# FFN-in with the high weights in one 512-column matmul per k-tile, and one pool of PSUM banks

## The chip, the cores and the metric

The kernel runs on one core of a Trainium2 chip. The metric is the device time of one execution in microseconds (us), the median of several runs. TensorE (PE) multiplies, and its weight loads have a row of their own (PEld); VectorE (DVE) and ScalarE (ACT) do the elementwise work, GpSimd (POOL) a little of it, and the queue of SyncE (SP) issues the transfers from device memory. PSUM, where matmuls accumulate, has 8 banks; a bank holds 512 fp32 values for each of 128 partitions.

## The reference

Two layers, each `x + FFN`, a mixer, and `x + FFN` again, on 256 tokens of 1024 channels in fp32. What the change touches is the first product of the four feed-forward stages (two per layer, `ffa` and `ffb`):

```
def swiglu(h, w_in, w_out):                      # h [256, 1024], w_in [1024, 2*2816], w_out [2816, 1024]
    gate, up = jnp.split(h @ w_in, 2, axis=-1)
    return (jax.nn.silu(gate) * up) @ w_out
...
x = x + 0.5 * swiglu(rms_norm(x, ffa_norm[l]), ffa_w_in[l], ffa_w_out[l])
```

The mixer between them runs three branches (a low-rank attention, a gated delta rule with a causal convolution, a block attention), gates them and projects them back.

## The kernel before

Each fp32 product is made of three fp32r matmuls. A weight block of 512 KB is loaded into `raw`, ACT casts it to its high part `wh` (line 258, two casts of 512 columns) and DVE subtracts to get the low part `wl` (line 259); the activations are kept as high and low parts as well, in tiles [128, k-tile, part, token]. A product is then high x high, high x low and low x high.

There are two forms of the product. `chunk` (lines 278 to 280) is token-major: 128 tokens are the stationary operand, the weights stream through in 512 columns. It makes the first 512 gate columns of each FFN, FFN-out, and many mixer products. `tiles` (lines 306 to 308) is channel-major: a 128x128 piece of the weights is stationary, the 256 tokens stream. It makes all other columns of FFN-in, 20 tiles of 256 columns per feed-forward stage with 8 k-tiles each, and the mixer's gates and branches. One PSUM bank holds the whole tile, two column halves (`c`) of 256 tokens. Its three matmuls per column half and k-tile have 256 columns each:

```
mm(o, wh[:, k, v], xh, ...)     # L306
mm(o, wh[:, k, v], xl, ...)     # L307
mm(o, wl[:, k, v], xh, ...)     # L308
```

The mixer's convolution tiles (lines 914 and 915) already have the other form: `wh` streams against the high and the low tokens in one matmul of 512 columns, `wl` against the high tokens in one of 256, and the two halves of the bank are added at eviction, an ACT copy (line 924) and a DVE add (line 926).

In FFN-in a gate tile is evicted by `silu2`: ACT's tanh from the bank (line 428) and a DVE operation on both (line 429). An up tile is multiplied by its gate from the bank (DVE, line 460), then split by an ACT cast (line 324) and a DVE subtraction (line 325), which gives `HT[j]` for FFN-out.

The PSUM banks are three pools: `acc` with 3 banks for the weights' products, `pm` with 3 for attention and the delta rule, `tp` with 2 for transposes. `held` counts the banks in use: `acc()` lets other chains go first until fewer than 3 are held, `hold()` keeps chains of `pm` below 2. The order of the work is the order of emission, taken as the priority by a scheduler that places the instructions on each engine; chains beside the weights are generators that yield for a number of events. Weights are split at least LEAD = 3 steps ahead, and 7 pairs `wh`, `wl` exist.

Of the kernel before, what the change touches and what calls it, by code (L numbers as in the profile page):

```python
# [8 lines left out]
F32 = mybir.dt.float32  # L9
# [27 lines left out]
NACC, NTP = 3, 2  # L37
# for how many events a chain lets others go first
Y_ATT, Y_INV, Y_DMA, LAG, START, G_AHEAD = 3, 3, 8, 2, 40, 20
# the mixer's weights: L low-rank products, C conv channels, M block attention, Z delta rule's z, G gates, B branches  # L40
# [32 lines left out]
class Step:  # L73
    """One group of weights: load() -> (DRAM blocks, k-tiles, columns), use(t, wh, wl) per token half;
    joint: used once, for both halves, by a generator."""
# [5 lines left out]
class Kern:  # L81
    def __init__(self, ctx, tc, ins, out):
        self.tc, self.nc, self.ins, self.out = tc, tc.nc, ins, out
        self.sb = ctx.enter_context(tc.tile_pool(name="sb", bufs=1))
        self.dr = ctx.enter_context(tc.tile_pool(name="dr", bufs=1, space=bass.MemoryType.DRAM))
        self.ps = ctx.enter_context(tc.tile_pool(name="ps", bufs=1, space=bass.MemoryType.PSUM))
        self.n = 0
        self.gens, self.clock = [], 0
        self.held = {"acc": 0, "pm": 0}

# [16 lines left out]
    def pm(self):  # L107
        return self.ps.tile([128, 512], F32, name=self.nm("pm"), tag="pm", bufs=8 - NACC - NTP)

    def acc(self):  # L110
        """a bank for the weights' products; its last reader calls done("acc")"""
        self.until(lambda: self.held["acc"] < NACC)
        self.held["acc"] += 1
        return self.ps.tile([128, 512], F32, name=self.nm("acc"), tag="acc", bufs=NACC)

    def hold(self):
        """a chain that keeps a bank over a yield first waits for this, and ends with done("pm")"""
        while self.held["pm"] >= 7 - NACC - NTP:
            yield 1
        self.held["pm"] += 1  # L120
# [5 lines left out]
    # A generator is a chain of work beside the weights; it yields, for so many events, where its  # L126
    # next piece has to wait for another engine.
# [55 lines left out]
    def layer_params(self, l):  # L183
# [12 lines left out]
        # rope tables with the gains folded in: [t][A | B]  # L196
# [39 lines left out]
    def fetch(self, split, most=NRAW):  # L236
        """start the loads that have room; split one more k-tile pair's half, if it is not far ahead"""
# [27 lines left out]
    def chunk(self, src, nk, n, xget, epi, before=None):  # L265
        """[tokens, n] = x @ w, token-major, per token half; src(k0, k1) -> DRAM blocks."""
# [19 lines left out]
    def tiles(self, w, nk, a0, both, epi, before=None):  # L286
        """256 columns of x @ w, channel-major, both token halves at once: bank [128, 2 column tiles, 256 tokens]"""
        acc = []

        def step(g):  # L290
# [3 lines left out]
            def use(wh, wl):  # L294
# [6 lines left out]
                for c in range(2):  # L301
                    o = ps[:, c * 256:(c + 1) * 256]
                    v = slice(c * 128, (c + 1) * 128)
                    for k in range(4):
                        xh, xl = both(4 * g + k)
                        mm(o, wh[:, k, v], xh, start=(g == 0 and c == 0 and k == 0), stop=False, skip_group_check=True)  # L306
                        mm(o, wh[:, k, v], xl, start=False, stop=False, skip_group_check=True)  # L307
                        mm(o, wl[:, k, v], xh, start=False, stop=(4 * g + k == nk - 1), skip_group_check=True)  # L308
                    if c == 0:
                        yield  # L310
# [16 lines left out]
    def rsq(self, out, ss, add, mul=1.0):  # L327
        """out = (mul * ss + add) ** -0.5"""
# [11 lines left out]
    def half_T(self, n):  # L340
        """storage for n k-tiles of one token half, split: (tile, dst)"""
# [12 lines left out]
    def norm(self, t, gain, put, lag):  # L354
        """rms norm of x's half t, transposed and split; put(c, y) does that for 512 channels"""
# [33 lines left out]
    def xboth(self, k):  # L389
        for t in range(NH):  # L390
            self.until(lambda: (t, k // 4) in self.XR)
        return self.X[k // 2][:, k % 2, 0, :], self.X[k // 2][:, k % 2, 1, :]
# [22 lines left out]
    def ffn(self, l, name, norm_after):  # L415
# [9 lines left out]
        def silu2(dst, ps):  # L425
            """dst = 2 * silu(ps)"""
# [5 lines left out]
        def epi_first(t, ps):  # L432
            """the first 512 gates come token-major, for each half of the tokens"""
# [13 lines left out]

        def epi_gate(j):
            def f(ps):
                SG[j] = self.b2().rearrange("p (k c) -> p k c", k=2)  # L450
                silu2(SG[j], ps)
                self.done("acc")
                return
                yield
            return f

        def epi_up(j):
            def f(ps):
                h = self.b2().rearrange("p (k c) -> p k c", k=2)
                nc.vector.tensor_tensor(h, SG[j], ps.rearrange("p (k c) -> p k c", k=2), op=OP.mult)  # L460
                self.done("acc")
# [17 lines left out]
    def rope(self, dst, src, tab, H, d):  # L479
        """dst = src * A + swap(src) * B over H heads; src may be in PSUM"""  # L480
# [9 lines left out]
    def sumsq(self, src):  # L490
        """sum of src[:, h, :] ** 2, by the scalar engine alone"""
# [85 lines left out]
    def gdn(self, ready, sil, beta, g, zs, oT):  # L577
        """the gated delta rule over two chunks of 128 tokens, four heads at once; sil(0..2): 2*silu of the conv of
        q, k, v, channel-major, there when ready(i)"""
# [41 lines left out]
        # The l2 norms of q and k stay factors of the token: with r = 1 / |k|, k = r k',  # L621
        # beta (1 + tril(beta k k^T D))^-1 (v - e k S) = beta r (1 + tril(k' k'^T D beta r^2))^-1 (v / r - e k' S)
# [65 lines left out]
        def invert(c):  # L688
# [46 lines left out]
            # the last level joins two blocks of 64  # L735
# [95 lines left out]
    def mixer(self, l, norm_after):  # L831
# [8 lines left out]
        # c_q, c_kv, k_rope, b, a  # L840
        def epi_c(t, ps):
# [37 lines left out]
            # g = -exp(a_log) * softplus(a + dt_bias), softplus(x) = max(x, 0) + log(1 + exp(-|x|))  # L879
# [19 lines left out]
        # q, k, v of the delta rule: channel-major, 128 channels at a time  # L899
        def conv_tile(i, h):  # L900
# [6 lines left out]
            def use(wh, wl):  # L907
# [4 lines left out]
                for k in range(8):  # L912
                    xh, xl = self.xboth(k)
# [26 lines left out]
        # low-rank attention: queries, then keys and values  # L940
# [54 lines left out]
        def use_kv(t, wh, wl):  # L995
            xh, xl = cget(t, 2)
            for hg in range(2):
                self.until(lambda: self.held["pm"] < 7 - NACC - NTP)
# [10 lines left out]
        def attend():  # L1009
            """both softmax branches, one after the other"""  # L1010
# [23 lines left out]
        # block attention: one block holds the whole sequence, so every routed block is masked and only the  # L1034
        # causal part in the block is left
# [30 lines left out]
        # gates, the delta rule's z and the branches  # L1066
# [19 lines left out]
        def gates(n):  # L1086
            r = []
            for j in range(4):
                r += self.tiles(w_in, 8, GATE + n * D + j * 256, self.xboth, epi_gate(n, j))
# [19 lines left out]
        def branch(n):  # L1109
            r = []  # L1110
            both = lambda k: (d["oT", n][k // 2][:, k % 2, 0, :], d["oT", n][k // 2][:, k % 2, 1, :])
            for j in range(4):
                r += self.tiles(ins["w_branch"][l, n], 4, j * 256, both, epi_b(n, j),
# [20 lines left out]
    def phase(self, steps):  # L1134
        """the first half of the tokens runs SKEW steps ahead of the second"""
        n = len(steps)
        ev = [(0, i) for i in range(SKEW)]
# [26 lines left out]
    def run(self):  # L1164
# [29 lines left out]
        with self.tc.manual_schedule():  # L1194
            # the first half's norm and the first weights, in the order in which they arrive
# [26 lines left out]
        for p in phases:  # L1222
            self.phase(p)
# [22 lines left out]
```

## Time and profile before

| | |
|---|---|
| median of 3 runs | 1360.8 us (1360.14 to 1361.75) |
| span of the profiled execution, first to last instruction | 1358.5 us |
| PE / PEld busy | 1333.1 us (98%) / 1218.3 us (90%) |
| DVE / ACT / POOL busy | 881.6 (65%) / 734.3 (54%) / 122.4 us (9%) |
| data moved by the DMA engines | 231.39 MB, mean 170 GB/s |
| granted TensorE clock | full speed in all 40 slices |

The profile gives the profiled execution's span and no other time of it; the median is 2.3 us above that span. Matmuls are pipelined: the duration of one (283 ns for 256 columns) runs on while the next ones have started, so the rate is read from the distance of two starts. Busy PE is the union of these durations, so it is high wherever PE is fed at all. Idle time of DVE and ACT costs nothing as long as PE does not wait for them.

### The profile page before, as it was taken

How to read it: one execution, taken by the hardware profiler on the slowest of the kernel's cores; microseconds unless marked ns; L12 is line 12 of the kernel's file. 1: busy time of each engine (PE TensorE's matmuls, PEld its weight loads, DVE VectorE, ACT ScalarE, POOL GpSimd, SP SyncE). 2: the span in 40 equal slices, each digit the busy share in tenths (PEclk: the TensorE clock that was granted, in tenths of full speed). 3: DMA queues.
4: the chain of work that ended last, by engine and by line, in shares of the span. 5: the costliest groups of instructions: out<-in, count | busy, mean ns of one | idle time of the engine just before them, and what ended most of it. 6: DMA issues, size and time to landing. Idle time of an engine off the chain costs nothing.

```text
span 1358.5 us, 23647 instructions
## 1 busy us (share of the span) xinstructions
PE 1333.1 (98%) x9066; PEld 1218.3 (90%) x9066; DVE 881.6 (65%) x1730; ACT 734.3 (54%) x1623; POOL 122.4 (9%) x157
## 2 busy tenths in 40 slices
PE   6999999999999999999999999999999999999998
PEld 5999888788899979998889998887889999899987
DVE  6666458898557676555575555588875576765552
ACT  6444447776655465444464444477757644644432
POOL 0010003711101000000000000044120000000000
PEclk9999999999999999999999999999999999999999
DMA  8866565566343656565666565555554445666552
GB/s 274 231 217 185 172 186 134 171 174 172 109 125 110 187 169 208 182 185 173 198 187 197 180 183 174 165 156 161 166 147 119 136 131 171 186 186 185 180 174 67
DMA packets 207568, 231.39 MB, mean 170 GB/s; under 512 B 15616, under 2 KB 166112, under 8 KB 207456
## 3 DMA queue, kind: packets, MB, share of 16 engines
q1 hardware_dynamic: 207456, 229.89, 56.7%
q8 instruction: 71, 1.16, 0.3%
q14 instruction: 41, 0.34, 0.1%
HBM read 227.11 MB, written 2.75 MB: 169 GB/s over the span
## 4 chain that ended last, share of the span: by engine, by line
PE 91%; DVE 3%; POOL 3%; ACT 1%; DMA 1%; issue 1%; SPq 0%; DVEq 0%; ACTq 0%; POOLq 0%
PE acc L306 16%; PE acc L307 16%; PE acc L308 16%; PE acc L278 10%; PE acc L280 10%; PE acc L279 10%; PE acc L914 3%; PE pm L523 2%; PE acc L915 1%; POOL s L331 1%; DMA raw<-in_ffa_w_in 1%; DVE wl L259 1%; POOL s L330 1%; PE tp L336 1%; PE pm L562 1%
## 5 line engine op out<-in xcount | busy, mean ns | idle before, releaser
L259 DVE TENSOR_TENSOR wl<-raw,wh 128x512 fp32r<-128x512 f32 (+1 forms) x844 | 555.7, 687 | 295.4 <-ACT wh L258 295.2
L258 ACT CAST wh<-raw 128x512 fp32r<-128x512 f32 (+1 forms) x844 | 487.9, 618 | 479.2 <-issue 323.4
L306 PE MATMUL acc<-q,wh 128*128 128x256 f32 x1856 | 530.3, 286 | 0.0
L307 PE MATMUL acc<-q,wh 128*128 128x256 f32 x1856 | 525.4, 283 | 2.0 <-DVE q L325 2.0
L308 PE MATMUL acc<-q,wl 128*128 128x256 f32 x1856 | 525.4, 283 | 0.0
L307 PEld LDWEIGHTS acc<-q,wh 128*128 128x128 f32 x1856 | 355.9, 192 | 3.7 <-DVE q L325 2.8
L306 PEld LDWEIGHTS acc<-q,wh 128*128 128x128 f32 x1856 | 355.9, 192 | 2.7 <-issue 1.0
L308 PEld LDWEIGHTS acc<-q,wl 128*128 128x128 f32 x1856 | 355.8, 192 | 0.0
L278 PE MATMUL acc<-wh,q 128*128 128x512 f32 (+2 forms) x656 | 258.4, 394 | 1.5 <-ACT q L324 1.4
L280 PE MATMUL acc<-wh,q 128*128 128x512 f32 (+2 forms) x656 | 255.8, 390 | 0.0
L279 PE MATMUL acc<-wl,q 128*128 128x512 f32 (+2 forms) x656 | 255.1, 389 | 0.0
L278 PEld LDWEIGHTS acc<-wh,q 128*128 128x128 f32 x656 | 123.7, 189 | 26.8 <-ACT q L324 2.4
L280 PEld LDWEIGHTS acc<-wh,q 128*128 128x128 f32 x656 | 123.5, 188 | 26.3 <-DVE q L325 2.1
L279 PEld LDWEIGHTS acc<-wl,q 128*128 128x128 f32 x656 | 123.6, 188 | 21.8
L914 PE MATMUL acc<-q,wh 128*128 128x512 f32 x192 | 70.9, 407 | 0.0
L358 POOL TENSOR_TENSOR s<-s,mhalf 128x1 f32<-128x1 f32 x12 | 8.3, 692 | 643.6 <-DVE s L351 643.6
L915 PE MATMUL acc<-q,wl 128*128 128x256 f32 x192 | 54.0, 281 | 0.0
L460 DVE TENSOR_TENSOR d<-d,acc 128x512 f32<-128x512 f32 x36 | 24.8, 688 | 41.9 <-PE acc L308 41.9
L914 PEld LDWEIGHTS acc<-q,wh 128*128 128x128 f32 x192 | 36.1, 188 | 8.6 <-issue 0.7
L535 ACT ACTIVATE d<-pm,s,s 128x128 f32<-128x128 f32 (+1 forms) x64 | 32.1, 509 | 21.2 <-DVE s L531 20.6
L331 POOL TENSOR_TENSOR s<-s,mhalf 128x4 f32<-128x4 f32 (+2 forms) x32 | 36.9, 1155 | 2.5
L915 PEld LDWEIGHTS acc<-q,wl 128*128 128x128 f32 x192 | 36.3, 189 | 0.4
(197 smaller groups left out, 1066.5 us busy)
## 6 DMA issues: line engine op xcount, KB each, us to landing
raw<-in_w_in SPq DMA_DIRECT2D x104, 512.0 KB
raw<-in_ffa_w_in SPq DMA_DIRECT2D x88, 512.0 KB
raw<-in_ffb_w_in SPq DMA_DIRECT2D x88, 512.0 KB
raw<-in_ffa_w_out SPq DMA_DIRECT2D x44, 512.0 KB
raw<-in_ffb_w_out SPq DMA_DIRECT2D x44, 512.0 KB
raw<-in_w_branch SPq DMA_DIRECT2D x24, 512.0 KB
raw<-in_w_out SPq DMA_DIRECT2D x16, 512.0 KB
raw<-in_w_in SPq DMA_DIRECT2D x8, 416.0 KB
```

Of the source, the lines that this page charges most:

```text
L258: nc.scalar.copy(s.wh[:, v], s.raw[:, v])
L259: nc.vector.tensor_sub(s.wl[:, v], s.raw[:, v], s.wh[:, v].bitcast(F32))
L278: mm(o, xh, wh[:, j, :], start=(k == 0), stop=False)
L279: mm(o, xh, wl[:, j, :], start=False, stop=False)
L280: mm(o, xl, wh[:, j, :], start=False, stop=(k == nk - 1))
L306: mm(o, wh[:, k, v], xh, start=(g == 0 and c == 0 and k == 0), stop=False, skip_group_check=True)
L307: mm(o, wh[:, k, v], xl, start=False, stop=False, skip_group_check=True)
L308: mm(o, wl[:, k, v], xh, start=False, stop=(4 * g + k == nk - 1), skip_group_check=True)
L331: g.tensor_tensor(out, out, self.mhalf[:, 0:out.shape[-1]], op=OP.pow)
L535: nc.scalar.activation(P[:, h, :], ps[:, h, :], AF.Exp, scale=rqs[:, h:h + 1], bias=nb[:, h:h + 1], accum_out=sm[:, h:h + 1])
L914: mm(p, wh[:, k, :], self.X[k // 2][:, k % 2], start=(k == 0), stop=False, skip_group_check=True)
L915: mm(p[:, 0, :], wl[:, k, :], xh, start=False, stop=(k == 7), skip_group_check=True)
```

## The change

In FFN-in, `tiles` now uses two banks, one per column half. For each k-tile it issues one matmul of 512 columns, `wh` against high and low tokens, and one of 256 columns, `wl` against the high tokens into the bank's first half. A bank is evicted by the new `whole`: an ACT copy of its second half and, an event later, a DVE add of its first half. The gate's tanh and DVE operation and the up tile's multiplication then read SBUF. The old function stays as `narrow` for the mixer's gates and branches. `acc` and `pm` become one pool of 6 banks; up to 4 `acc` banks may be held in a feed-forward stage, 3 in the mixer, and 2 `pm` banks by `hold()` as before. The rest of the diff is comments taken out and the moving operand passed as one tile instead of two.

```
-NACC, NTP = 3, 2
+NTP = 2
+BANKS = 8 - NTP
     def pm(self):
-        return self.ps.tile([128, 512], F32, name=self.nm("pm"), tag="pm", bufs=8 - NACC - NTP)
+        return self.ps.tile([128, 512], F32, name=self.nm("pm"), tag="bank", bufs=BANKS)
     def acc(self):
-        self.until(lambda: self.held["acc"] < NACC)
+        self.until(lambda: self.held["acc"] < self.nacc)
         self.held["acc"] += 1
-        return self.ps.tile([128, 512], F32, name=self.nm("acc"), tag="acc", bufs=NACC)
+        return self.ps.tile([128, 512], F32, name=self.nm("acc"), tag="bank", bufs=BANKS)
     def hold(self):
-        while self.held["pm"] >= 7 - NACC - NTP:
+        while self.held["pm"] >= BANKS - 4:
...
     def tiles(self, w, nk, a0, both, epi, before=None):
+                for c in range(2):
+                    if g == 0:
+                        acc[c] = self.acc()
+                    ps = acc[c]
+                    v = slice(c * 128, (c + 1) * 128)
+                    for k in range(4):
+                        x2 = both(4 * g + k)
+                        last = 4 * g + k == nk - 1
+                        mm(ps.rearrange("p (s c) -> p s c", s=2), wh[:, k, v], x2, start=(g == 0 and k == 0), stop=False,
+                           skip_group_check=True)
+                        mm(ps[:, 0:256], wl[:, k, v], x2[:, 0, :], start=False, stop=last, skip_group_check=True)
+                    if 4 * g + 4 == nk:
+                        self.spawn(epi(c, ps))
+                    if c == 0:
+                        yield
...
+        def whole(dst, ps):
+            nc.scalar.copy(dst, ps[:, 256:512])
+            yield 1
+            nc.vector.tensor_tensor(dst, dst, ps[:, 0:256], op=OP.add)
+            self.done("acc")
         def epi_gate(j):
-            def f(ps):
-                SG[j] = self.b2().rearrange("p (k c) -> p k c", k=2)
-                silu2(SG[j], ps)
-                self.done("acc")
+            def f(c, ps):
+                if c == 0:
+                    SG["raw", j] = self.b2().rearrange("p (k c) -> p k c", k=2)
+                g = SG["raw", j]
+                yield from whole(g[:, c, :], ps)
+                if c == 1:
+                    yield 1
+                    SG[j] = self.b2().rearrange("p (k c) -> p k c", k=2)
+                    silu2(SG[j], g.rearrange("p k c -> p (k c)"))
         def epi_up(j):
-                nc.vector.tensor_tensor(h, SG[j], ps.rearrange("p (k c) -> p k c", k=2), op=OP.mult)
-                self.done("acc")
+                h = SG["up", j]
+                yield from whole(h[:, c, :], ps)
+                if c == 0:
+                    return
+                yield 1
+                while j not in SG:
+                    yield 1
+                nc.vector.tensor_tensor(h, h, SG[j], op=OP.mult)
...
-    def phase(self, steps):
+    def phase(self, steps, nacc):
...
-            self.phase(p)
+            self.phase(p, 3 if i % 3 == 1 else 4)
```

**On PE, inside FFN-in.** Before, at the border of two tiles of the first feed-forward stage (`acc_638` and `acc_705` are banks, `q_96` to `q_99` the tokens, `wh` and `wl` the weights' parts, in brackets the semaphores that a row waits for):

```order
L306 MATMUL acc_638<-q_99,wh_562 128x256
L307 MATMUL acc_638<-q_99,wh_562 128x256
L308 MATMUL acc_638<-q_99,wl_563 128x256
L306 MATMUL acc_705<-q_96,wh_598 128x256 [waits DVE_49]
L307 MATMUL acc_705<-q_96,wh_598 128x256
L308 MATMUL acc_705<-q_96,wl_599 128x256
```

The same border in the changed program:

```order
L309 MATMUL acc_710<-q_99,wh_635 128x512
L311 MATMUL acc_710<-q_99,wl_636 128x256
L309 MATMUL acc_757<-q_96,wh_663 128x512 [waits DVE_49]
L311 MATMUL acc_757<-q_96,wl_664 128x256
...
L309 MATMUL acc_814<-q_96,wh_663 128x512 [waits DVE_49]
L311 MATMUL acc_814<-q_96,wl_664 128x256
```

Three matmuls of a k-tile have become two, and a tile opens two banks instead of one, with a wait at the first matmul of each.

**On DVE, inside FFN-in.** Before, around an up tile (its multiplication is L460) and its split (L325):

```order
L460 TENSOR_TENSOR d_558<-d_487,acc_497 128x512 [waits DVE_49,PE_49]
L259 TENSOR_TENSOR wl_668<-raw_526,wh_667 128x512 [waits DMAHW3_49,Activation_49]
L259 TENSOR_TENSOR wl_668<-raw_526,wh_667 128x512 [waits Activation_49]
L325 TENSOR_TENSOR q_579<-d_558,q_579 128x2x256 [waits Activation_49]
L259 TENSOR_TENSOR wl_702<-raw_560,wh_701 128x512 [waits DMAHW5_49,PE_49,Activation_49]
```

The same in the changed program (L486 is the new add, L512 the multiplication, L359 the split, L261 the weights' low part):

```order
L486 TENSOR_TENSOR d_619<-d_619,acc_580 128x256 [waits Activation_49]
L261 TENSOR_TENSOR wl_726<-raw_605,wh_725 128x512 [waits DMAHW6_49,PE_49,Activation_49]
L486 TENSOR_TENSOR d_619<-d_619,acc_592 128x256 [waits Activation_49]
L261 TENSOR_TENSOR wl_726<-raw_605,wh_725 128x512 [waits Activation_49]
L512 TENSOR_TENSOR d_619<-d_619,d_601 128x512 [waits DVE_49]
L261 TENSOR_TENSOR wl_754<-raw_633,wh_753 128x512 [waits DMAHW0_49,PE_49,Activation_49]
L359 TENSOR_TENSOR q_675<-d_619,q_675 128x2x256 [waits Activation_49]
L261 TENSOR_TENSOR wl_754<-raw_633,wh_753 128x512 [waits Activation_49]
```

Two adds per tile have come between the subtractions, each behind an ACT copy.

**On PE, in the first mixer.** Before, the second token half of a 384-column product (`acc_2532`) stands inside another product and its first row waits:

```order
L280 MATMUL acc_2430<-wh_2363,q_2160 128x512
L278 MATMUL acc_2430<-wh_2403,q_2161 128x512
L278 MATMUL acc_2532<-wh_2442,q_2297 128x384 [waits DVE_49,PE_49]
L279 MATMUL acc_2532<-wl_2443,q_2297 128x384
L280 MATMUL acc_2532<-wh_2442,q_2297 128x384
...
L279 MATMUL acc_2430<-wl_2404,q_2161 128x512
L946 MATMUL tp_2540<-ident,d_2494 128x128 [waits DVE_49,Activation_49]
```

In the changed program its two halves follow each other, and the wait is at a later product (`acc_2374`):

```order
L282 MATMUL acc_2291<-wh_2123,q_2086 128x384
L280 MATMUL acc_2321<-wh_2231,q_2086 128x384
...
L282 MATMUL acc_2321<-wh_2231,q_2086 128x384
L280 MATMUL acc_2219<-wh_2152,q_1949 128x512
...
L280 MATMUL acc_2374<-wh_2266,q_1947 128x512 [waits PE_49]
L997 MATMUL tp_2329<-ident,d_2283 128x128 [waits DVE_49,Activation_49]
```

The pieces of work are the same and stand in another order; the mixer's PE list has 8 more rows with a wait than before (130 for 122 in the first mixer).

## Rows read from the trace of the kernel before

**Rows 1.** The head of the profile's page and the table of engines: busy time, share of the span, instructions; and the granted clock by fortieths of the span.
```profile
span 1358.5 us, 23647 instructions
PE 1333.1 (98%) x9066; PEld 1218.3 (90%) x9066; DVE 881.6 (65%) x1730; ACT 734.3 (54%) x1623; POOL 122.4 (9%) x157
PEclk9999999999999999999999999999999999999999
```

**Rows 2.** The costliest groups of instructions: line, engine, operation, tiles, shapes, count; then busy us, mean ns of one; then idle time of the engine before them.
```profile
L306 PE MATMUL acc<-q,wh 128*128 128x256 f32 x1856 | 530.3, 286 | 0.0
L307 PE MATMUL acc<-q,wh 128*128 128x256 f32 x1856 | 525.4, 283 | 2.0 <-DVE q L325 2.0
L308 PE MATMUL acc<-q,wl 128*128 128x256 f32 x1856 | 525.4, 283 | 0.0
L306 PEld LDWEIGHTS acc<-q,wh 128*128 128x128 f32 x1856 | 355.9, 192 | 2.7 <-issue 1.0
L914 PE MATMUL acc<-q,wh 128*128 128x512 f32 x192 | 70.9, 407 | 0.0
L915 PE MATMUL acc<-q,wl 128*128 128x256 f32 x192 | 54.0, 281 | 0.0
```

**Rows 3.** The timeline of PE in the first FFN-in, start in us, duration in us: the first and the last of 35 matmuls of 256 columns in unbroken order.
```profile
99.80 0.28 PE L306 MATMUL acc<-q,wh 128*128 128x256 f32 x1
...
103.88 0.28 PE L307 MATMUL acc<-q,wh 128*128 128x256 f32 x1
```

**Rows 4.** The timeline of PE in FFN-out of the first feed-forward stage: the first and the last of 15 matmuls of 512 columns in unbroken order.
```profile
169.67 0.39 PE L278 MATMUL acc<-wh,q 128*128 128x512 f32 x1
...
172.84 0.39 PE L280 MATMUL acc<-wh,q 128*128 128x512 f32 x1
```

**Rows 5.** The timeline of PE in a convolution tile of the first mixer, 8 pairs of a 512- and a 256-column matmul: the second pair's first matmul, the last pair's first, and the next product.
```profile
246.73 0.39 PE L914 MATMUL acc<-q,wh 128*128 128x512 f32 x1
246.96 0.28 PE L915 MATMUL acc<-q,wl 128*128 128x256 f32 x1
...
248.81 0.39 PE L914 MATMUL acc<-q,wh 128*128 128x512 f32 x1
249.04 0.28 PE L915 MATMUL acc<-q,wl 128*128 128x256 f32 x1
```

**Rows 6.** The same in another convolution tile, behind 256-column matmuls of the gates: the first and the last of its 8 pairs.
```profile
300.35 0.40 PE L914 MATMUL acc<-q,wh 128*128 128x512 f32 x1
300.58 0.28 PE L915 MATMUL acc<-q,wl 128*128 128x256 f32 x1
...
302.82 0.40 PE L914 MATMUL acc<-q,wh 128*128 128x512 f32 x1
```

**Rows 7.** Busy time of the engines in stretches that lie inside the FFN-in of the four feed-forward stages: stretch, its us, then busy us and count of PE, PEld, DVE, ACT, POOL, the granted clock, the DMA share and GB/s.
```profile
32.00:88.00 56.00, 56.00 (x469) 56.00 (x468) 36.64 (x61) 27.74 (x52) 7.61 (x18) 1.00 0.80 240
515.00:618.00 103.00, 103.00 (x861) 103.00 (x860) 62.91 (x100) 50.22 (x90) 0.00 (x0) 1.00 0.61 189
702.00:808.00 106.00, 106.00 (x886) 106.00 (x885) 64.99 (x103) 51.38 (x92) 0.00 (x0) 1.00 0.63 192
1182.00:1288.00 106.00, 106.00 (x886) 106.00 (x885) 64.97 (x103) 51.36 (x92) 0.00 (x0) 1.00 0.61 187
```

**Rows 8.** Groups of DVE and ACT in the stretch 515 to 618 us, with the idle time before them and what ended it.
```profile
L259 DVE TENSOR_TENSOR wl<-raw,wh 128x512 fp32r<-128x512 f32 x72 | 47.2, 687 | 30.2 <-ACT wh L258 30.2
L460 DVE TENSOR_TENSOR d<-d,acc 128x512 f32<-128x512 f32 x8 | 5.5, 688 | 8.1 <-PE acc L308 8.1
L258 ACT CAST wh<-raw 128x512 fp32r<-128x512 f32 x72 | 41.8, 618 | 53.1 <-issue 51.7 <-PE acc L307 1.4
```

**Rows 9.** The eviction of the convolution tiles, durations in ns, least, median and most.
```profile
L924 ACT COPY d<-acc x24: 348/367/411, 249.8 to 1081.5; 128x256 f32<-128x256 f32 x24
L926 DVE TENSOR_TENSOR d<-acc,d x24: 385/418/426, 252.4 to 1082.7; 128x256 f32<-128x256 f32 x24
```

**Rows 10.** What PE waited for, the whole span: us in total, times, longest us; and one stretch that holds most of the first mixer, with columns as in Rows 7.
```profile
PE tp L336 <- DVE d L362: 12.2, 8, 9.4
PE tp L946 <- DVE d L1057: 3.9, 4, 1.2
PE acc L307 <- DVE q L325: 2.0, 4, 0.8
PE tp L946 <- DVE d L990: 1.5, 2, 0.7
215.00:460.00 245.00, 241.14 (x1684) 216.43 (x1683) 179.80 (x431) 157.61 (x410) 54.54 (x63) 1.00 0.52 148
```

More of the change, by code (lines that the diff above doesn't have):

```diff
@@ L89, in __init__ @@
         self.held = {"acc": 0, "pm": 0}
+        self.nacc = 3
     def nm(self, s):
@@ L286, in tiles, with step, load, use @@
     def tiles(self, w, nk, a0, both, epi, before=None):
+        acc = {}
+        def step(g):
+            def load():
+                return [w[g * 512:(g + 1) * 512, a0:a0 + 256].rearrange("(k p) n -> p k n", p=128)], 4, 256
+            def use(wh, wl):
+                if g == 0 and before:
+                    before()
+                mm = self.nc.tensor.matmul
+                for c in range(2):
[13 more added lines that the diff above has]
+                        yield
+            return Step(load, use, joint=True)
+        return [step(g) for g in range(nk // 4)]
+    def narrow(self, w, nk, a0, both, epi, before=None):
         acc = []
@@ L304, in use @@
                     for k in range(4):
-                        xh, xl = both(4 * g + k)
+                        x2 = both(4 * g + k)
+                        xh, xl = x2[:, 0, :], x2[:, 1, :]
                         mm(o, wh[:, k, v], xh, start=(g == 0 and c == 0 and k == 0), stop=False, skip_group_check=True)
@@ L391, in xboth @@
             self.until(lambda: (t, k // 4) in self.XR)
-        return self.X[k // 2][:, k % 2, 0, :], self.X[k // 2][:, k % 2, 1, :]
+        return self.X[k // 2][:, k % 2]
     def residual(self, c, scale, norm_after):
@@ L446, in epi_first, with f @@
                 SG[0], SG[1] = g[:, 0:2, :], g[:, 2:4, :]
-        def epi_gate(j):
-            def f(ps):
-                SG[j] = self.b2().rearrange("p (k c) -> p k c", k=2)
-                silu2(SG[j], ps)
-                self.done("acc")
-                return
-                yield
+        def whole(dst, ps):
[3 more added lines that the diff above has]
+            self.done("acc")
+        def epi_gate(j):
+            def f(c, ps):
[7 more added lines that the diff above has]
+                    silu2(SG[j], g.rearrange("p k c -> p (k c)"))
             return f
         def epi_up(j):
-            def f(ps):
-                h = self.b2().rearrange("p (k c) -> p k c", k=2)
-                nc.vector.tensor_tensor(h, SG[j], ps.rearrange("p (k c) -> p k c", k=2), op=OP.mult)
-                self.done("acc")
+            def f(c, ps):
+                if c == 0:
+                    SG["up", j] = self.b2().rearrange("p (k c) -> p k c", k=2)
+                h = SG["up", j]
+                yield from whole(h[:, c, :], ps)
+                if c == 0:
+                    return
[3 more added lines that the diff above has]
+                nc.vector.tensor_tensor(h, h, SG[j], op=OP.mult)
                 yield 1
@@ L912, in use @@
                 for k in range(8):
-                    xh, xl = self.xboth(k)
+                    xh = self.xboth(k)[:, 0, :]
                     mm(p, wh[:, k, :], self.X[k // 2][:, k % 2], start=(k == 0), stop=False, skip_group_check=True)
@@ L997, in use_kv @@
             for hg in range(2):
-                self.until(lambda: self.held["pm"] < 7 - NACC - NTP)
+                self.until(lambda: self.held["pm"] < BANKS - 4)
                 self.held["pm"] += 1
@@ L1088, in gates @@
             for j in range(4):
-                r += self.tiles(w_in, 8, GATE + n * D + j * 256, self.xboth, epi_gate(n, j))
+                r += self.narrow(w_in, 8, GATE + n * D + j * 256, self.xboth, epi_gate(n, j))
             return r
@@ L1110, in branch @@
             r = []
-            both = lambda k: (d["oT", n][k // 2][:, k % 2, 0, :], d["oT", n][k // 2][:, k % 2, 1, :])
+            both = lambda k: d["oT", n][k // 2][:, k % 2]
             for j in range(4):
-                r += self.tiles(ins["w_branch"][l, n], 4, j * 256, both, epi_b(n, j),
+                r += self.narrow(ins["w_branch"][l, n], 4, j * 256, both, epi_b(n, j),
                                 before=(lambda: self.until(lambda: ("o", n) in d)) if j == 0 else None)
@@ L1131, in mixer @@
         return steps
-    def phase(self, steps):
+    def phase(self, steps, nacc):
         n = len(steps)
+        self.nacc = nacc
         ev = [(0, i) for i in range(SKEW)]
@@ L1221, in run @@
         self.spawn(params())
-        for p in phases:
-            self.phase(p)
+        for i, p in enumerate(phases):
+            self.phase(p, 3 if i % 3 == 1 else 4)
 _INS = ['x', 'ffa_norm', 'ffa_w_in', 'ffa_w_out', 'mix_norm', 'w_in', 'mla_cq_norm', 'mla_ckv_norm', 'mla_w_uq',
```

## The prediction

> **What bounds the kernel now.** I read the table of engines first. PE is busy for 98% of the span at the full granted clock, DVE for 65% and ACT for 54% [rows 1]. Busy PE is not PE at its peak, so the next view is what PE waited for: 12.2 us before the transposes of the norm, 9.4 of them once, at the start, and a few single microseconds in the mixers [rows 10]. No wait of PE for a weight, a transfer or a bank in FFN-in is among them. Then the stretches inside FFN-in: in 103 us PE starts about 861 matmuls, one per 120 ns, while DVE works 62.91 us and ACT 50.22 [rows 7]. DVE's idle time there ends with ACT's cast, and ACT's ends with nothing that the profile shows [rows 8]; both are paced by PE, which frees the weight buffers. So in FFN-in the end is set by how many matmuls PE issues and by the distance of their starts, and by nothing else.
>
> **The distance of two starts.** In the groups a 256-column matmul lasts 283 ns and a 512-column one 407 [rows 2]. Taken as costs, these would make three times 283 against 407 plus 281, 161 ns less per k-tile; but they overlap. The timeline gives the rate. 34 intervals between 256-column starts take 103.88 - 99.80 = 4.08 us, 120.0 ns each [rows 3]. 14 intervals between 512-column starts take 172.84 - 169.67 = 3.17 us, 226.4 ns each [rows 4]. 256 more columns thus cost 106.4 ns, and 120.0 - 106.4 = 13.6 ns is left as the cost of one more matmul, whatever its width. That is the whole prize: the change streams the same 768 columns per k-tile and saves one matmul.
>
> **The price of the new pair.** The convolution tiles already run the new form, so the pair need not be put together from other shapes. It runs at two speeds, each steady within a tile. In one tile six pairs take 248.81 - 246.73 = 2.08 us, 346.7 ns a pair [rows 5], which is the sum of the two distances above. In another seven take 302.82 - 300.35 = 2.47 us, 352.9 ns [rows 6]. Both tiles have the same shapes; they differ in what PE ran before. I have no row that says which of the two a long unbroken run of pairs settles in. The four FFN-ins have interruptions of their own at their heads (the transposes of the first gates), and I expect some of both, so I take the middle, 350 ns, and keep both as ends.
>
> **The change, part by part.**
>
> 1. *Matmuls removed.* The 1856 k-tile groups of lines 306 to 308 [rows 2] hold FFN-in and the mixer. Per mixer, 12 gate tiles of 16 groups and 12 branch tiles of 8 are 288, and 576 for two layers, which keep their form. FFN-in has 4 stages x 20 tiles x 2 column halves x 8 k-tiles = 1280 groups. Each falls from 360.0 to 350 ns: 1280 x 10.0 = 12.8 us. Ends: 1280 x (360.0 - 352.9) = 9.1 us and 1280 x (360.0 - 346.7) = 17.0 us. All of it lies on the path.
> 2. *Weight loads removed.* One per group goes too. A load lasts 192 ns [rows 2], yet matmuls start every 120 ns with PEld busy all the time [rows 7]; loads run beside matmuls and their cost is already in the distances. No term.
> 3. *Eviction added.* Per tile of 256 columns two ACT copies (367 ns) and two DVE adds (418 ns) are added [rows 9]; tanh, multiplication and split stay, with SBUF for PSUM as their source. A tile takes 16 x 0.36 = 5.76 us now, so the 103 us hold 17.9 tiles. DVE goes from 62.91 to 62.91 + 17.9 x 0.836 = 77.9 us, ACT from 50.22 to 50.22 + 17.9 x 0.734 = 63.4 us [rows 7], and the stretch shrinks to about 100. So 78% and 63%: both keep a margin, and the weights are split steps ahead of their use, so a late add is not a late weight. Term 0. If that cover is gone, see the third rival.
> 4. *Banks.* A tile opens two banks half a step apart. A bank is opened again some tiles later out of six, and its eviction takes 367 + 418 ns plus queueing; a column half of a step takes 4 x 350 ns = 1.4 us. The up tile's mult and split come later than before, by one add and one or two events; FFN-out begins with k-tile 0, so the last `HT` is wanted ten steps later. Term 0.
> 5. *The mixer.* Its products are unchanged and PE idles for 3.9 of 245 us there [rows 10]. The shared pool moves rows on PE, adds 8 waiting rows per mixer, and removes some interruptions of products. PE's idle time bounds the gain: 2 us for each mixer. The longest wait there is 1.2 us [rows 10]; two or three such would cost 3. I take 0, with -3 to +5 us for both mixers.
> 6. *Transfers.* The same bytes in 3% less time: FFN-in goes from 189 to about 195 GB/s, and the first FFN-in already runs at 240 [rows 7]. Term 0.
>
> Sum: -12.8 us. The profiled span would become 1358.5 - 12.8 = 1345.7, and the median, 2.3 us above the span now, 1360.8 - 12.8 = **1348.0 us**. With both ends of the pair and of the mixer: 1360.8 - 17.0 - 3 = 1340.8 to 1360.8 - 9.1 + 5 = 1356.7.
>
> **A rule to weigh.** The rows show 13.6 ns for a matmul beyond its columns [rows 3, 4]. The Trainium skill, "TensorE: Matmul & The Clock Gate", section "Back-to-back issue gap", gives the isolated distance at the full clock as columns by 2.4 GHz plus 2.5 ns. By it the sum would be 1280 x 2.5 = 3.2 us and the time an estimated 1357.6. It does not fit 120.0 ns for 256 columns; I go by the rows.
>
> **The rivals.**
>
> - *The removed matmul was nearly free.* In place of the fixed cost, the distance of the 256-column starts could be set by something that the new pair keeps, such as a load of weights that the shorter matmul no longer covers. For it: PEld is busy in all of FFN-in [rows 7], and the slower pair already gives back 6.2 of the 13.3 ns [rows 6]. Against it: in neither tile do the pairs average above 353 [rows 5, 6]. At 357 ns the gain is 1280 x 3 = 3.8 us and the time 1357.0. Chance 0.06. The skill's formula, above, would come out near this time.
> - *Slower: PE waits for banks in the mixer.* A product's first matmul may now get a bank that an attention or delta-rule chain holds until ACT or DVE has read it, where before it had three of its own. PE is in order, so all behind it waits. 8 more waiting rows in each of two mixers at the longest single wait of 1.2 us [rows 10] are 19.2 us, and 1360.8 - 12.8 + 19.2 = 1367.2. It decides from 12.8 / 16 = 0.8 us per added wait. For it: the order has changed over the whole mixer, and chains there are long. Against it: a wait in the list is mostly one that is already met; 122 waiting rows cost under 4 us now, and the number of banks that may be held is the same. Chance 0.07.
> - *DVE becomes the bound of FFN-in.* In 103 us DVE waits 30.2 us for casts and 8.1 for PE [rows 8]. If none of that could shrink, the adds would come on top: 103 + 15.0 = 118.0 us, 15% more in 461 us of FFN-in, some 67 us, and 1415. For it: each add stands behind a copy that waits for PE, and blocks the subtractions behind it. Against it: ACT's idle time is time ahead of need, not work, and shrinks once DVE is late. It decides only when DVE's 78% and what it must really wait for pass the whole stretch. Chance 0.03.
> - *Both speeds as one.* All of FFN-in in the faster pair gives 1343.8, all in the slower 1351.7. These are the ends of the forecast and no case of their own.
>
> **How the numbers follow.** The forecast with its ends has 0.82, the free matmul 0.06, bank waits 0.07, DVE 0.03; 0.02 is left for a mixer that gains more than its idle time. The range takes in the ends of the pair and most of the mixer's, and the free matmul's time: 1342 to 1357. A measurement of this kernel can tell about 0.2% (2.7 us) from no change, so same is 1358.1 to 1363.5. Faster: the forecast, most of the free matmul and the remainder, 0.88. Same: the rest of the free matmul and small bank waits, 0.05. Slower: large bank waits and DVE, 0.07.
>
> **What would show it.** Right: 512- and 256-column starts in FFN-in alternate with 347 or 353 ns from pair to pair; each FFN-in is 2.3 to 4.3 us shorter; DVE busy near 78% in it, with PE's idle time unchanged; the mixers within a few microseconds of before. Wrong: pairs of 357 ns or more; idle time of PE that ends with DVE's add or the weights' low part in FFN-in; a mixer that is longer by more than 5 us, with first matmuls of products waiting.

## The result

| | before | changed |
|---|---|---|
| median of the runs made with the result | 1361.3 us (1360.1 to 1363.2, 4 runs) | 1353.5 us (1350.5 to 1354.1, 4 runs) |
| span of the profiled execution | 1358.5 us | 1348.5 us |

The ratio is 0.9941 (95% interval 0.9928 to 0.9954): 7.8 us less where 12.8 were forecast, inside the range of 1342 to 1357. The profiled execution of the changed kernel is its quickest, 1350.5 us, so its span shows 10.0 us of gain where the median shows 7.8. That difference between one execution and the next turns out to be half of the explanation.

### The profile page after: what moved, and what is told of

Read it like the earlier page. It is cut to its first block, busy times and chain, and to the rows that moved or that the text cites. A ratio compares the mean times of both kernels' runs of the same rounds, so it can differ in the third digit from the quotient of the medians.

```text
span 1348.5 us, 21398 instructions
## 1 busy us (share of the span) xinstructions
PE 1320.3 (98%) x7786; PEld 1150.3 (85%) x7786; DVE 937.4 (70%) x1890; ACT 786.9 (58%) x1783; POOL 117.9 (9%) x157
## 4 chain that ended last, share of the span: by engine, by line
PE 92%; DVE 3%; ACT 2%; POOL 1%; DMA 1%; issue 1%; SPq 0%; DVEq 0%; ACTq 0%; POOLq 0%
PE acc L309 22%; PE acc L311 11%; PE acc L280 10%; PE acc L282 10%; PE acc L281 10%; PE acc L340 5%; PE acc L341 5%; PE acc L342 5%; PE acc L965 3%; PE pm L574 2%; PE acc L966 1%; ACT wh L260 1%; DMA raw<-in_ffa_w_in 1%; DVE wl L261 1%; PE tp L370 1%; PE pm L613 1%
## 5 line engine op out<-in xcount | busy, mean ns | idle before, releaser
L261 DVE TENSOR_TENSOR wl<-raw,wh 128x512 fp32r<-128x512 f32 (+1 forms) x844 | 563.2, 687 | 265.7 <-ACT wh L260 265.4
L260 ACT CAST wh<-raw 128x512 fp32r<-128x512 f32 (+1 forms) x844 | 497.2, 619 | 389.7 <-issue 147.4
L309 PE MATMUL acc<-q,wh 128*128 128x512 f32 x1280 | 449.3, 396 | 0.0
L311 PE MATMUL acc<-q,wl 128*128 128x256 f32 x1280 | 359.2, 281 | 0.0
L309 PEld LDWEIGHTS acc<-q,wh 128*128 128x128 f32 x1280 | 240.1, 188 | 55.8
L311 PEld LDWEIGHTS acc<-q,wl 128*128 128x128 f32 x1280 | 242.4, 189 | 0.5
L340 PE MATMUL acc<-q,wh 128*128 128x256 f32 x576 | 168.3, 292 | 0.0
L341 PE MATMUL acc<-q,wh 128*128 128x256 f32 x576 | 163.2, 283 | 0.4 <-DVE q L359 0.4
L342 PE MATMUL acc<-q,wl 128*128 128x256 f32 x576 | 163.0, 283 | 0.0
L340 PEld LDWEIGHTS acc<-q,wh 128*128 128x128 f32 x576 | 110.3, 192 | 1.8 <-issue 1.0
L341 PEld LDWEIGHTS acc<-q,wh 128*128 128x128 f32 x576 | 110.3, 191 | 1.2 <-DVE q L359 0.8
L342 PEld LDWEIGHTS acc<-q,wl 128*128 128x128 f32 x576 | 110.1, 191 | 0.1
L965 PE MATMUL acc<-q,wh 128*128 128x512 f32 x192 | 70.5, 406 | 0.0
L486 DVE TENSOR_TENSOR d<-d,acc 128x256 f32<-128x256 f32 x160 | 66.5, 416 | 5.3 <-ACT d L484 5.3
L484 ACT COPY d<-acc 128x256 f32<-128x256 f32 x160 | 58.8, 368 | 18.9 <-PE acc L311 18.8
```

What stands on the lines that cost most here:

```text
L260: nc.scalar.copy(s.wh[:, v], s.raw[:, v])
L261: nc.vector.tensor_sub(s.wl[:, v], s.raw[:, v], s.wh[:, v].bitcast(F32))
L309: mm(ps.rearrange("p (s c) -> p s c", s=2), wh[:, k, v], x2, start=(g == 0 and k == 0), stop=False, skip_group_check=True)
L311: mm(ps[:, 0:256], wl[:, k, v], x2[:, 0, :], start=False, stop=last, skip_group_check=True)
L486: nc.vector.tensor_tensor(dst, dst, ps[:, 0:256], op=OP.add)
L965: mm(p, wh[:, k, :], self.X[k // 2][:, k % 2], start=(k == 0), stop=False, skip_group_check=True)
```

## The profile after, and where the time went

The head of the page and its table of engines, of the changed kernel, against [rows 1]:

```profile
span 1348.5 us, 21398 instructions
PE 1320.3 (98%) x7786; PEld 1150.3 (85%) x7786; DVE 937.4 (70%) x1890; ACT 786.9 (58%) x1783; POOL 117.9 (9%) x157
```

PE has 1280 matmuls fewer, DVE 160 instructions and 56 us more, ACT 160 and 53 us more. These are the counts of the sum. The groups of the new pair and of its evictions (busy us, mean ns of one, idle time before), against [rows 2]:

```profile
L309 PE MATMUL acc<-q,wh 128*128 128x512 f32 x1280 | 449.3, 396 | 0.0
L311 PE MATMUL acc<-q,wl 128*128 128x256 f32 x1280 | 359.2, 281 | 0.0
L486 DVE TENSOR_TENSOR d<-d,acc 128x256 f32<-128x256 f32 x160 | 66.5, 416 | 5.3 <-ACT d L484 5.3
L484 ACT COPY d<-acc 128x256 f32<-128x256 f32 x160 | 58.8, 368 | 18.9 <-PE acc L311 18.8
```

Add and copy last what the convolution's did, 416 and 368 ns for 418 and 367 [rows 9]. Now stretches of the four FFN-ins, columns as in [rows 7]:

```profile
34.00:84.00 50.00, 50.00 (x285) 43.38 (x284) 39.00 (x73) 30.88 (x64) 8.08 (x18) 1.00 0.77 241
530.00:610.00 80.00, 80.00 (x464) 70.59 (x463) 60.05 (x108) 49.78 (x102) 0.00 (x0) 1.00 0.61 190
715.00:795.00 80.00, 80.00 (x455) 69.36 (x454) 59.88 (x107) 48.82 (x100) 0.00 (x0) 1.00 0.60 187
1195.00:1275.00 80.00, 80.00 (x464) 70.59 (x463) 60.06 (x109) 49.77 (x102) 0.00 (x0) 1.00 0.61 191
```

PE never idles in any of them, and DVE is busy for 75 to 78%, as worked out. But equal stretches hold 464 matmuls in the second and fourth stage and 455 in the third. The timeline of PE says why: the start of one wide matmul and of another 21 pairs later, in the second stage,

```profile
519.95 0.39 PE L309 MATMUL acc<-q,wh 128*128 128x512 f32 x1
...
527.23 0.39 PE L309 MATMUL acc<-q,wh 128*128 128x512 f32 x1
```

7.28 us by 21 are 346.7 ns a pair, exactly the short cycle of [rows 5]. The third stage runs the long one of [rows 6], and so does the first:

```profile
696.14 0.40 PE L309 MATMUL acc<-q,wh 128*128 128x512 f32 x1
...
696.49 0.40 PE L309 MATMUL acc<-q,wh 128*128 128x512 f32 x1
...
696.84 0.40 PE L309 MATMUL acc<-q,wh 128*128 128x512 f32 x1
...
697.20 0.40 PE L309 MATMUL acc<-q,wh 128*128 128x512 f32 x1
...
702.50 0.40 PE L309 MATMUL acc<-q,wh 128*128 128x512 f32 x1
```

The long cycle is not a pair that is slower each time: it repeats after three pairs, of 350, 350 and 360 ns, and 18 pairs take 6.36 us, 353.3 ns each. The lengths of the stages agree. From the start of a stage's first transposes to the next norm's (in FFN 1 from the transposes of its first gates, in FFN 4 to the end) FFN 1 to 4 went from 179.5, 190.0, 189.4 and 193.6 us to 177.2, 185.8, 187.4 and 189.5. That is 2.3, 4.2, 2.0 and 4.1 less, together 12.6 us.

What is missing lies in the mixers. The stretch of the whole first mixer, before and after:

```profile
203.80:494.60 290.80, 286.22 (x1941) 255.98 (x1941) 214.23 (x494) 182.36 (x468) 57.69 (x70) 1.00 0.53 151
```

```profile
201.50:493.60 292.10, 286.13 (x1941) 256.29 (x1941) 213.13 (x494) 182.23 (x467) 55.51 (x70) 1.00 0.53 150
```

The same 1941 matmuls and the same busy time, in 1.3 us more; the second mixer likewise (874.1 to 1164.8, now 866.8 to 1158.9). So it is idle time of PE, and the waits name it (us in total, times, longest), against [rows 10]:

```profile
PE tp L370 <- DVE d L396: 12.0, 8, 9.3
PE tp L669 <- DMA q<-zd: 4.5, 4, 1.4
PE tp L997 <- DVE d L1108: 4.2, 4, 1.4
...
PE pm L821 <- ACT d L837: 1.4, 2, 0.7
...
PE acc L341 <- DVE q L359: 0.4, 2, 0.2
```

A wait for `q<-zd` has come, 4.5 us in all, and one of 2.0 us at a gate product has gone to 0.4. `zd` is where the delta rule's block inverses go through device memory and come back regrouped. PE now stands at their transposes until the reload has landed.

## The experiments

Each ran beside the kernel before on its chip, whose medians there were 1360.2 to 1361.3 us.

**1. The changed kernel again** (no edit).

Expected: 

> The changed kernel once more, nothing edited. Theory A (each FFN-in stage falls into one of two steady cycles of the pair, 347 or 353.5 ns, and which one is not fixed by the program): the profile shows the four stages in another mix of the two than 353.8, 347.0, 353.6, 346.9; every stage that changes its cycle moves the span by 2.1 us, so times lie between 1346 (all fast) and 1356 us (all slow), median 1353. Theory B (the cycle is fixed by what the program runs before the stage): the same four values again, span 1348.5, and the scatter of the times comes from elsewhere.

Measured: 1352.8 us (1350.9 to 1355.1). The profiled execution is one of 1355.0 us, span 1352.9, and its last three stages are all in the long cycle:

```profile
530.00:610.00 80.00, 80.00 (x454) 69.39 (x454) 59.84 (x107) 48.69 (x99) 0.00 (x0) 1.00 0.59 188
715.00:795.00 80.00, 80.00 (x454) 69.41 (x454) 59.76 (x107) 48.95 (x99) 0.00 (x0) 1.00 0.60 188
1195.00:1275.00 80.00, 80.00 (x454) 69.31 (x454) 59.75 (x107) 48.83 (x99) 0.00 (x0) 1.00 0.59 188
```

454 where two of these stages had 464 before, in the same program. Its first stage holds 285 in 50 us as in the first profile, the long cycle too. Two stages changed their cycle; the span moved by 4.4 us, and 2 x 320 x 6.6 ns are 4.2. Theory A holds: which cycle a stage runs is not a property of the program. Nor is it one of the chip alone: these five times come from one chip, all at the full granted clock, and spread over 4.2 us. The nine executions of the changed kernel, 1350.5 to 1355.1 us, lie where two to four stages in the long cycle put them; only these two were profiled.

**2. Only the pool.** FFN-in as before, `acc` and `pm` in one pool:

```
-steps += self.tiles(w_in, 8, j * 256, self.xboth, epi_gate(j))        # and the up tiles
+steps += self.narrow(w_in, 8, j * 256, self.xboth, epi_gate(j))       # with the old epi_gate, epi_up
```

Expected: 

> Only the pool: acc and pm in one pool of 6 banks, FFN-in in the old form with three 256-column matmuls and the old evictions. Theory A (the shared pool moves rows in the mixer and each mixer gets 1.35 us longer): 1361.3 + 2.7 = 1364.0 us, mixers of 292.1 us, PE waits for the delta rule's reloads from device memory (q<-zd) of 4 to 5 us in all. Rival (the pool is neutral, the mixers got longer because they started at another moment behind a shorter FFN): within 1 us of before, mixers of 290.8.

Measured: 1362.5 us against 1360.2 (ratio 1.0017, interval 1.0008 to 1.0026), mixers of 292.2 and 292.1 us. The same wait:

```profile
PE tp L652 <- DMA q<-zd: 4.3, 4, 1.3
```

The pool alone costs what the mixers lost. Its PE order in the mixer is row for row that of the changed kernel, and differs from that of before at 230 of 1941 places in the first mixer. The reload of the second token half is issued at 332.7 us and wanted at 336 there; before, it was issued at 332.6 and wanted at 341.2. The timelines of PE show what stands in between: here the transposes come earlier in a list of the same work.

```profile
334.64 0.63 PE L652 MATMUL tp<-ident,q 128*128 128x128 f32 x4 [1.34 <-DMA q<-zd]
...
337.04 0.63 PE L652 MATMUL tp<-ident,q 128*128 128x128 f32 x4 [0.88 <-DMA q<-zd]
```

and before:

```profile
337.39 0.60 PE L618 MATMUL tp<-ident,q 128*128 128x128 f32 x4
...
341.19 0.60 PE L618 MATMUL tp<-ident,q 128*128 128x128 f32 x4
```

That the order does it, and not the shared banks as such, is read from the wait and these rows; a shared pool with the old order was not tried.

**3. Only the new form**, with `acc` and `pm` apart as before:

```
-tag="bank", bufs=BANKS)        # pm and acc
+tag="pm", bufs=3)              # tag="acc", bufs=3)
-self.phase(p, 3 if i % 3 == 1 else 4)
+self.phase(p, 3)
```

Expected: 

> Only the new form: FFN-in with the 512-column matmul and the new evictions, acc and pm apart with 3 banks each as before, 3 acc banks held at most. Theory A: the mixers are as before (290.8 us each) and FFN-in keeps its gain of 12.8 us (8.5 if all four stages run the slow cycle, 17 if all run the fast one): span 1345.8, time 1348 to 1352. Rival (the two banks of a tile need the larger pool, PE waits for the third bank's eviction): 80 tiles x 0.4 us = 32 us, 1380, with idle time of PE that ends with the DVE add.

Measured: 1351.1 us (1349.8 to 1352.4; ratio 0.9931, 0.9919 to 0.9943). The FFN gain stands without the larger pool; three banks are enough, and no wait for a bank shows. One part of the expectation failed: the mixers took 292.3 and 292.2 us in the profiled execution, though their PE order is that of before and their waits are those of before. The granted clock fell there, after two pauses of PE (0.73 and 1.20 us):

```profile
261.01 0.61 PE L997 MATMUL tp<-ident,d 128*96 128x128 f32 x4 [0.73 <-DVE d L1041]
263.27 0.85 PE L997 MATMUL tp<-ident,d 128*128 128x128 f32 x4 [1.20 <-DVE d L1108]
...
265.84 0.63 PE L965 MATMUL acc<-q,wh 128*128 128x512 f32 x1
266.27 0.41 PE L966 MATMUL acc<-q,wl 128*128 128x256 f32 x1
266.48 0.61 PE L965 MATMUL acc<-q,wh 128*128 128x512 f32 x1
```

```profile
255.00:275.00 20.00, 18.08 (x92) 15.03 (x91) 16.77 (x39) 14.46 (x46) 12.24 (x19) 0.91 0.54 137
```

A pair takes 640 ns there, at the 1.2 GHz level; it cost 1.5 us in each mixer. The pauses are those of before, whose profile keeps 2.4 GHz through them; it is an accident of single executions. Some of before's own have a mean clock below 1 as well and are 1 to 3 us longer. So the profiled execution hides the pool's price; the times (1351.1 against 1352.8 and 1353.5) show 1.7 to 2.4 us of it, with such falls and both cycles mixed in. Experiment 7 has the pools apart at the full clock and settles it.

The profile shows one thing more, in the first stage:

```profile
29.36 0.40 PE L309 MATMUL acc<-q,wh 128*128 128x512 f32 x1
...
85.52 0.40 PE L309 MATMUL acc<-q,wh 128*128 128x512 f32 x1
...
85.97 0.26 PE L225 MATMUL tp<-ident,cw 48*128 48x48 f32 x1
...
86.61 0.40 PE L309 MATMUL acc<-q,wh 128*128 128x512 f32 x1
...
133.96 0.40 PE L309 MATMUL acc<-q,wh 128*128 128x512 f32 x1
```

162 pairs in 56.16 us are 346.7 ns each, the short cycle; then a single transpose of the parameters (line 225) comes between, and the 134 pairs behind it take 47.35 us, 353.4 each, the long one. So a cycle lasts until something interrupts the pairs, and can change there.

**4. Wide matmuls together.** Per column half and step, four wide ones and then four narrow ones:

```
+for k in range(4): mm(ps..., wh[:, k, v], both(4 * g + k), ...)
+for k in range(4): mm(ps[:, 0:256], wl[:, k, v], both(4 * g + k)[:, 0, :], ...)
```

Expected: 

> The changed kernel, but in each column half of a step the four 512-column matmuls come first and then the four 256-column ones. Theory A (the slow cycle belongs to the alternation of the two widths; equal widths in a row run at 227 and 120 ns): four k-tiles take 4 x 346.7 = 1387 ns in all four stages, 4.3 us less than the profiled run of the changed kernel: span 1344, time 1346 to 1348, with less scatter. Rival (a switch of width costs time whenever it comes, or each stage still picks a cycle): slow stages remain, span 1348 to 1352.

Measured: 1352.1 us (1351.3 to 1353.8), the same as the changed kernel. The theory failed in its number and its rival was nearer: all four stages run alike, but at some 351 ns per k-tile. In the trace the wide matmuls behind a switch start 228 to 236 ns apart, 234 in the mean, and do not settle at 227 within four.

**5. Three matmuls in the new banks.** The changed kernel, with `wh` against `xh` into the bank's first half, `wh` against `xl` into its second and `wl` against `xh` into the first, 256 columns each:

```
-mm(ps.rearrange("p (s c) -> p s c", s=2), wh[:, k, v], x2, ...)
+mm(ps[:, 0:256], wh[:, k, v], x2[:, 0, :], ...)
+mm(ps[:, 256:512], wh[:, k, v], x2[:, 1, :], ...)
```

Expected: 

> The changed kernel with its two banks per tile, its evictions and its pool, but with three matmuls of 256 columns per k-tile as before. Theory A (the whole FFN gain is the removed matmul, evictions are free, the pool costs about 2.3 us): FFN-in back at 120 ns per matmul, 1360.2 + 2.3 = 1362.5 us. Rival (the new evictions or the two banks cost time in FFN-in): more than 1364 us, with PE waiting for DVE's add in FFN-in.

Measured: 1363.4 us against 1360.6 (ratio 1.0018, 1.0009 to 1.0027). One stretch of FFN-in, to be held against the same stretch above:

```profile
715.00:795.00 80.00, 80.00 (x669) 80.00 (x669) 59.24 (x105) 47.86 (x98) 0.00 (x0) 1.00 0.61 187
```

669 matmuls in 80 us are 120 ns each, with all new evictions in place. They cost nothing in FFN-in; what is left is the pool's 2 to 3 us, and the whole gain is the removed matmul, with the weight load that goes with it.

The pool's price can be higher in a single execution. In the first mixer of this profile PE stood 2.1 us at a stretch for the reload, in the second mixer of experiment 4's 2.0 us. Behind it the granted clock fell (0.79 over 8 us in both), and these mixers took 294.1 and 294.3 us.

**6. Every eviction twice.**

```
+more = self.b2()[:, 0:256]
+nc.scalar.copy(more, ps[:, 256:512])
 nc.scalar.copy(dst, ps[:, 256:512])
 yield 1
+nc.vector.tensor_tensor(more, more, ps[:, 0:256], op=OP.add)
 nc.vector.tensor_tensor(dst, dst, ps[:, 0:256], op=OP.add)
```

Expected: 

> The changed kernel with every eviction done twice: each bank is copied and added once more into a tile that nobody reads. Theory A (DVE and ACT have room in FFN-in): DVE rises by 160 x 0.416 = 67 us in all, from 76% to 91% of FFN-in, ACT by 59 us, and the time stays at 1350 to 1356 us, the spread of the two cycles. Rival (DVE is near its bound, its waits for casts cannot shrink): FFN-in longer by up to 15% of 76% less the 24% that is idle, some 20 to 60 us, with PE waiting for the weights' low part.

Measured: 1350.4 us (1349.4 to 1352.6). Two of its stretches:

```profile
530.00:610.00 80.00, 80.00 (x464) 70.53 (x463) 70.46 (x138) 57.70 (x130) 0.00 (x0) 1.00 0.62 191
715.00:795.00 80.00, 80.00 (x454) 69.38 (x454) 69.28 (x136) 56.35 (x128) 0.00 (x0) 1.00 0.61 188
```

DVE is busy for 87 to 88% (91 were expected) and PE still never idles. DVE's waits for casts shrank to make room (202.6 us in the whole span where the changed kernel has 265.7), so the rival of a bound by DVE has fallen. The two cycles are there again, 464 and 454.

**7. Wide, narrow, narrow, wide.** The new form with the pools apart, and one switch of width per k-tile:

```
+for f in (wide, slim) if k % 2 == 0 else (slim, wide):
+    f()
```

Expected: 

> The new form with the pools apart (as e_forms), and the pairs in turn wide, narrow, narrow, wide, so that there is one switch of width per k-tile instead of two. Theory A (the slow cycle's 6.6 ns per pair come from the switches of width, 3.3 each): 350 ns per pair or less in all four stages, time 1349 to 1351. Rival (what counts is the phase in which a stage is entered): pairs still at 347 or 353.5 from stage to stage.

(`e_forms` is experiment 3.) Measured: 1346.2 us (1345.5 to 1346.9; ratio 0.9893, 0.9878 to 0.9908), span 1343.3, below both kernels and below the expected 1349, with a scatter of 1.3 us instead of 4.6. The stretches of the last three stages agree to one matmul:

```profile
530.00:610.00 80.00, 80.00 (x462) 69.79 (x461) 61.23 (x109) 50.32 (x101) 0.00 (x0) 1.00 0.59 187
715.00:795.00 80.00, 80.00 (x461) 69.78 (x461) 61.33 (x109) 50.50 (x101) 0.00 (x0) 1.00 0.62 190
1195.00:1275.00 80.00, 80.00 (x461) 69.76 (x460) 60.50 (x108) 50.02 (x101) 0.00 (x0) 1.00 0.61 191
```

These are 348.3 ns a pair, 1.7 above the short cycle and 5 below the long one, and the first stage has the same. Theory A's price for a switch of width does not fit beside experiment 4: four k-tiles there have two switches and take 350.8 ns each, here they have four and take 348.3, and in the changed kernel eight and take 346.7 or 353.3.

The mixers, with the new form but the pools apart and the clock at its full 2.4 GHz:

```profile
200.00:490.60 290.60, 286.14 (x1941) 255.98 (x1941) 214.11 (x494) 182.17 (x468) 57.35 (x70) 1.00 0.52 151
862.60:1153.30 290.70, 286.23 (x1942) 255.98 (x1942) 213.17 (x490) 182.17 (x467) 50.20 (x55) 1.00 0.51 149
```

That is their length before, in before's order, without a wait for the reload. So the 1.4 us that each mixer lost are the pool's and not the new form's. Of the 7 us to the changed kernel some 2.9 are the pool, the rest the pairs.

**8. The kernel before again** (no edit).

Expected: 

> The kernel before, unedited, for a second profile. If the mixers' length is a property of the program, they take 290.8 us each again and FFN-in shows 120 ns per matmul in all four stages; if mixers differ from execution to execution by more than 1 us, the mixers' share of the change's cost has to be read with that spread.

Measured: 1360.6 us (1359.5 to 1362.0), span 1357.8; mixers of 290.7 and 290.7 us, FFN stages of 179.0, 190.1, 189.4 and 193.6. At the full clock the mixers' length is a property of the program, to 0.1 us in before's order (290.6 to 290.8 with experiment 7's), so 1.3 us in each can be read. In the shared pool's order, where PE waits for a transfer, the profiles at the full clock show 292.1 to 292.6.

**9. One width only.** The low weights also against high and low tokens:

```
-mm(ps[:, 0:256], wl[:, k, v], x2[:, 0, :], ...)
+mm(p2, wl[:, k, v], x2, ...)
```

Expected: 

> The new form with the pools apart (as e_forms), and the low weights too against high and low tokens: two matmuls of 512 columns per k-tile (the product low x low is added, which the others leave out). Theory A (a matmul costs its columns at 2.4 GHz plus 13.3 ns, and a stream of one width has one speed): 226.7 ns per matmul in all four stages, 453.3 per k-tile, 1280 x (453.3 - 360.3) = 119 us more than before, 1479.5 us with a scatter below 2 us. Rival (each stage still picks between two speeds): stages at 227 and at 230 ns or more, and times that differ by 4 us.

Measured: 1479.7 us (1478.8 to 1481.2), 0.2 above the expectation; the scatter is 2.4 us, not below 2. In the first stage,

```profile
34.00:84.00 50.00, 50.00 (x222) 41.42 (x221) 31.18 (x58) 24.94 (x50) 6.35 (x13) 1.00 0.59 187
```

222 matmuls in 50 us, the rate of the 512-column stream of [rows 4]; the other stages have the same distance. A stream of one width has one speed here; the two speeds belong to the mixture.

## Why the prediction was right, and what its size missed

1. *The cost of a matmul beyond its columns, 13.6 ns: right.* Experiment 5 takes the matmul back and the gain is gone; experiment 9 adds 256 columns to each pair and comes out at 1479.7 us where the same law, with 13.3 ns (the columns counted at 2.4 GHz), gave 1479.5. The rival of a nearly free matmul is out: the profiled execution gains 12.6 us in its FFNs. By the formula that the Trainium skill gives for an isolated matmul ("TensorE: Matmul & The Clock Gate", section "Back-to-back issue gap"), 2.5 ns beyond the columns, it would have been an estimated 3.2; the measurement decides.
2. *The pair at 347 or 353 ns, taken as 350: the two values right, the mixture mis-sized.* In the profiled execution two stages ran each, which makes the forecast's 12.8 us; that this one was profiled is chance. In another all four ran the long one, 8.6 us by 1280 x 6.7. The median sits between: 7.8 us of gain and the pool's 2.3 to 2.8 make about 10.3 us in FFN-in, 352 ns a pair. The prediction put the speed down to what PE ran before, and took the middle of two tiles for want of a row; behind the same instructions both came, and the mixture differs from execution to execution.
3. *Evictions at nothing: right* (experiments 5 and 6). DVE was forecast at 78% and is at 75 to 78%. *Weight loads at nothing* fits, but no run removes a load without its matmul: PEld is busy throughout the 256-column stream of experiment 5 and 83% of the time in the 512-column one of experiment 9, and the cost beyond the columns, these counted at 2.4 GHz, is 13.3 ns in both.
4. *The mixer at 0, with -3 to +5: the step that failed in size.* It measures +2.3 to +2.8 us (experiments 2 and 5; 2.9 by the mixers' lengths in experiment 7). The mechanism I had named for added cost, banks held by long chains, is not it: the waits that came are for a transfer. The new order of rows calls for a reload from device memory sooner after its issue, and PE, in order, stands. I had counted the rows that wait and not asked of each how far it now stands behind the transfer that it waits for.
5. *Transfers: right;* FFN-in runs at 187 to 191 GB/s, at 241 in the first stage, and waits for none.

Together, 12.8 forecast, less some 2.5 for the mixture and some 2.5 for the mixers, gives the measured 7.8. Only the mixers' part is measured by itself; the mixture's is what the median leaves, and lies between the two profiled executions.

What stays open is what sets the cycle. Entry from the same instructions gave both; in the first stage of experiments 3 and 6 the short one ends at a single interruption and the long one follows. The program of experiment 7 leaves the choice out rather than explaining it.

## What to carry to other kernels

Where PE is fed without a break, price a matmul by the distance of starts in the trace, never by its duration; here, in a stream of one width, every matmul costs its columns and 13 ns, and a wider one saves about that. When shapes alternate, look at several stretches, since the same program can run them at two speeds. A change that touches a pool moves the order in stages that it does not mean to touch: look there for transfers whose user has come nearer to their issue.

## What the runs showed of the hardware that was not expected

- A stream that alternates 512- and 256-column fp32r matmuls holds one of two steady rhythms (346.7 ns a pair, or 350, 350 and 360 in turn, 353.3 in the mean) for up to a whole stage of 110 us, with PE never idle and the granted clock full. It can change at a single interruption, and from one execution to another. Streams of one width, 227 or 120 ns, do not.
- Two narrow matmuls between two wide ones run at 348.3 ns per k-tile in all four stages, within 1.3 us over whole executions.
- The granted clock can fall to the 1.2 GHz level behind pauses of PE of 0.7 and 1.2 us in one execution and stay at 2.4 GHz behind the same pauses in another; a fall cost 1.5 us.
